# Gate projections computed with tokens on partitions and turned through DRAM, and a planner with other load times and finer tables

## The chip, the cores and the metric

The kernel runs on one core of a Trainium2 chip. The metric is device time in microseconds for one execution, here the median of three runs. All data is float32; the matmuls take operands split into a high and a low part (float32r), so that one product costs three matmuls.

## The reference, cut to what matters

Two layers act on 256 latent tokens of width 2048, with 256 context tokens beside them in the first. The first layer is the one that the change touches:

```python
p = h @ w_in                    # q, gate_a, z, k, v, xbc, dt
pc = hc @ w_in[:, base:]        # context: k, v, xbc, dt alone
ya = neighbourhood_attention(q, k, v, kc, vc, rpb) * jax.nn.silu(gate_a)
yb = gated_group_rmsnorm(y_ssd + d * lat[0], z, ssm_norm_g)   # uses y * silu(z)
out = jnp.concatenate([ya, yb], axis=-1) @ w_out
```

`gate_a` and `z` are 256 tokens by 2048 columns each. They exist for the latent tokens alone, while k, v and most of xbc exist for all 512. The attention output and the SSD output are kept with their channels on partitions and the tokens along the free dimension, so silu of both gates is needed in that layout too.

## The kernel before, in words

**Work and order.** The columns of the first projection are cut into four slices of 512 for each of q, gate (G), z (Z), k, v and x. The main program first runs a starting stage over eight pieces `j` of two 128-row blocks each: it makes the layer's modulation (`ada_gen`: small matmuls with `cpad`, then transposes, then A0 and S0), normalizes and modulates the tokens (`hH`, `hL`), and accumulates K, V, Q of slice 0 and B. Partial sums of K and V are added into `sz`, `gt` and `Vt`, which serve there as accumulators (`part_gen`, L830). Then come, slice by slice, `do_g`, `do_ssd`, `do_qk` and `do_gv`; heads of attention (`head_gen`) and SSD groups (`group_gen`) are emitted between the matmuls of the projections. The output projection and a second layer with a short convolution follow.

**Two forms of a projection.** `proj` calls `chunk`, which calls one of two forms for each 128-row block. `mm_ws` (kind 256 or 512) holds a 128x128 block of the weight and streams the tokens, so the result has channels on partitions. `mm_act` (kind "act") holds 128 tokens and streams 512 weight columns, so the result has tokens on partitions. For 256 tokens and a 512-column slice the first form takes, per row block, four column blocks by three matmuls of 256 columns; the second takes two token tiles by three matmuls of 512 columns. Q, K and V of the later slices run as "act" and are then turned: written to DRAM from the GpSimd queue (`kqd`, L1029), fetched back in 128-element pieces by four DMAs (`fetch`, L245) into the one buffer `PT0`, and transposed in 32x32 squares by VectorE (`blocks`, L250). The flag `dfree` hands out `PT0`, which the heads use as well for their probabilities.

**The gates before.** `do_g` and the end of `do_ssd` project G and Z with kind 256. `silu2_gen` (L1054) waits for `ok()`, which says that the previous slice's gate buffer is no longer read. Then it makes tanh on ScalarE (L1059), and on VectorE (L1061) it multiplies out of PSUM straight into `gt` or `sz`. Until `ok()` holds, the two PSUM banks of the projection stay taken.

**What sets the order.** While the program is written, the class `Plan` keeps a clock per engine and a time for each piece of each tile. A task is emitted where its inputs are ready by those clocks. Each engine then runs its instructions strictly in the order written. A load of weights is costed from its size and `RATE` and a fixed delay. Tables of times are kept in pieces of 128 elements (`keys`), so that two parts of `small` or `const` that are loaded at different times can share one entry. Weight loads are issued from SyncE (L428) whenever one of the buffers `raw` comes free; ScalarE makes the high part `wH` (L458), VectorE the low part `wL` (L465), up to three loads ahead of their use.

Of the kernel before, what the change touches and what calls it, by code (L numbers as in the profile page):

```python
# [10 lines left out]
AF = mybir.ActivationFunctionType  # L11
ALU = mybir.AluOpType
AX = mybir.AxisListType

D = 2048
KB = 16
EPS = 1e-6
COL_Q, COL_G, COL_Z, COL_K, COL_V, COL_X = 0, 2048, 4096, 6144, 8192, 10240
# [19 lines left out]
class Plan:  # L38


    NAMES = {"PE": "PE", "DVE": "DVE", "Activation": "ACT", "Pool": "POOL", "SP": "SP"}
    RATE = 270.0

    def __init__(self):
        self.t = dict.fromkeys(("PE", "DVE", "ACT", "POOL", "SP"), 0.0)
        self.w, self.r, self.last = defaultdict(float), defaultdict(float), defaultdict(float)
        self.dma = 0.0
        self.pool = (0.0, 0.0)

    def keys(self, ap):  # L50
        a, n = ap.ap, ap.tensor.name
        if type(ap.tensor).__name__ == "Tile" and not n.startswith("dram"):
            lo = ap.offset % a[0][0] if a[0][0] else ap.offset
            hi = lo + sum(abs(s) * (c - 1) for s, c in a[1:])
            return [(n, u) for u in range(lo // 128, hi // 128 + 1)]
        if n.startswith("in_") or n.startswith("out_"):
            return []
        hi = ap.offset + sum(abs(s) * (c - 1) for s, c in a)
        return [(n, u) for u in range(ap.offset // 256, hi // 256 + 1)]
# [38 lines left out]
    def add(self, b):  # L98
        i = b.ins
        e, op = self.NAMES[str(i.engine).split(".")[-1]], i.opcode  # L100
        ins = [x.bass_ap for x in i.ins if hasattr(x, "bass_ap")]
        outs = [x.bass_ap for x in i.outs if hasattr(x, "bass_ap")]
        ki, ko = [k for a in ins for k in self.keys(a)], [k for a in outs for k in self.keys(a)]
        s = self.t[e]
        for k in ki:
            s = max(s, self.w[k] + 60)
        for k in ko:
            s = max(s, 0.0 if e == "PE" or op == "DMACopy" else self.w[k] + 60, self.r[k] + 60)
        if op == "DMACopy":
            n = 4  # L110
            for _, c in outs[0].ap:
                n *= c
            self.t[e] = s + (1200 if e == "POOL" else 450)
            if e == "SP":
                self.dma = max(self.dma, s + 1000) + n / self.RATE
                done = free = self.dma + 1000
            else:
                done = free = max(self.dma, s + 1000) + n / self.RATE + 1500
            if any(a.tensor.name.startswith("dram") for a in ins + outs):
                done = free = done + 3000  # L120
        else:
            d, lat = self.cost(e, op, i, ins, outs)
            if e == "DVE" and not self.psum(ins + outs) and self.pool[0] <= s < self.pool[1]:
                s = self.pool[1]
            if e == "POOL":
                self.pool = (s, s + d)
            self.t[e] = s + d
            free, done = s + d, s + d + lat
        for k in ki:
            self.r[k] = max(self.r[k], free)  # L130
            self.last[k[0]] = max(self.last[k[0]], free)
        for k in ko:
            self.w[k] = max(self.w[k], done) if op == "DMACopy" else done
            self.last[k[0]] = max(self.last[k[0]], done)
        return b
# [36 lines left out]
def kernel(ctx: ExitStack, tc, x, cx, ada_w, ada_b, w_in, w_out, sc_in, sc_out, rpb, small, const,  # L172
# [8 lines left out]
    w_in, w_out, sc_in, sc_out = (Laid(w, n) for w, n in ((w_in, "w_in"), (w_out, "w_out"), (sc_in, "sc_in"), (sc_out, "sc_out")))  # L181
    V, S, G, T, DMA = nc.vector, nc.scalar, nc.gpsimd, nc.tensor, nc.sync
# [18 lines left out]
    def drt(shape, name):  # L201
        return dr.tile(list(shape), F32, name="dram_" + name)
# [38 lines left out]
    def fetch(dst, src):  # L241

        n = src.shape[0] // 32
        for b in range(4):
            E(G.dma_start(dst[32 * b:32 * b + 32].rearrange("p t (a x) -> p (t a) x", a=4),  # L245
                             bass.AP(tensor=src.tensor, offset=src.offset + 128 * b, ap=[[512, 32], [32 * 512, n], [1, 128]])))

    def blocks(o, i):

        E(V.transpose(o.rearrange("p k (a j) -> p a k j", a=4), i.rearrange("p (a k j) -> p a k j", a=4, k=4)))  # L250
# [7 lines left out]
    def spawn(q, gen, tmps=0, halves=0):  # L258
        q.append(Task(gen, tmps, halves))
# [127 lines left out]
    def give(pool, *bs):  # L387
        pool.extend(bs)
# [342 lines left out]
    def proj(nc_, kind, ps, nxt, leave=False):  # L731
        nb = 1024 // nc_
        for kb in range(0, KB, nb):
            if kb + 2 * nb >= KB:
                reserve[0] = nxt
            chunk(kb, kind, ps, kb == 0, kb + nb >= KB)
            if leave:
                free_rows[0] = kb + nb
        reserve[0] = 0
# [263 lines left out]
    def d_take(name):  # L1003
        dfree[0] = False
        return st([128, 2, 512], "PT0", name=name)
# [40 lines left out]
    def v_gen(a, ps):  # L1046
# [4 lines left out]
            give(free_b, ps[t])  # L1051
        got.add(("V", a))

    def silu2_gen(key, a, ps, dst, ok):  # L1054
        yield when(lambda: ok())
        for b in range(2):
            yield W_("ACT", ps[b])
            th = tmp()
            E(S.activation(th, ps[b], AF.Tanh, scale=0.5))  # L1059
            yield W_("DVE", th)  # L1060
            E(V.scalar_tensor_tensor(out=dst[:, 2 * b:2 * b + 2, :].rearrange("p b c -> p (b c)"), in0=th, scalar=1.0,  # L1061
                                     in1=ps[b], op0=ALU.add, op1=ALU.mult))
            give(free_t, th)
            give(free_b, ps[b])
        got.add((key, a))

    b0 = rpbs[0, :, :]
# [6 lines left out]
    def head_gen(a, h):  # L1074
# [59 lines left out]
        yield W_("POOL", ptd[hd])  # L1134
        give(free_t, sps[0], sps[1])
        yield ("cap", 0, 0)
        yield when(lambda: dfree[0] and (hd == 0 or ("d", hd - 1) in got))
        Dt = d_take(f"D{hd}")
        got.add(("d", hd))
        yield W_("POOL", ptd[hd])  # L1140
# [383 lines left out]

    def do_g(a, nxt):
        psG = banks(2)
        proj(512, 256, psG, nxt)
        spawn(urgent, silu2_gen("G", a, psG, gt, lambda: attn[0] >= 8 * a and (a or ("K", 0) in got)), 1)

    def do_ssd(s, nxt):  # L1530
        if s:
            psB = banks(2)
            proj(256, 512, psB, 1)
            spawn(urgent, make_b(s, psB), 3)
        psC, = banks(1)
        proj(256, 256, [psC], 4)
        spawn(urgent, make_c(s, psC), 0, 2)
        psX = banks(4)
        proj(512, 512, psX, 2)
        for gi in range(2):  # L1540
            spawn(urgent, make_x(s, gi, psX[2 * gi:2 * gi + 2]), 3)
        psZ = banks(2)
        proj(512, 256, psZ, nxt)
        spawn(urgent, silu2_gen("Z", s, psZ, sz, lambda: ssd_done[0] >= 2 * s and ("K", 0) in got), 1)
        for gi in range(2):
            spawn(side, group_gen(s, gi), 3, 4)

# [456 lines left out]
```

## Time and profile before

| | |
|---|---|
| three runs | 1768.23, 1772.86, 1772.92 us; median 1772.86 |
| profiled execution | 1762.67 us; span of its instructions 1760.9 us |
| granted TensorE clock, mean | 0.999 |
| TensorE busy | 1728.3 us, 98% of the span |
| VectorE, ScalarE, GpSimd busy | 1292.8, 785.3, 191.0 us |
| moved by DMA | 412.50 MB, mean 234 GB/s |

A row of the profile names engine, line, operation, and output and input tiles with buffer numbers left out. For a matmul the moving operand is named first: `bank<-hH,wH 128x256` streams 256 tokens against a held block of the weight, and `bank<-wH,hH 128x512` streams 512 weight columns against 128 held tokens. Matmuls are pipelined, so the time from one row's start to the next row's start tells their pace, and the duration of a row is longer than that. A bracket behind a row of the timeline gives the engine's idle time ahead of it and the engine that ended it.

### The profile page before, as it was taken

How to read it: one execution, taken by the hardware profiler on the slowest of the kernel's cores; microseconds unless marked ns; L12 is line 12 of the kernel's file. 1: busy time of each engine (PE TensorE's matmuls, PEld its weight loads, DVE VectorE, ACT ScalarE, POOL GpSimd, SP SyncE). 2: the span in 40 equal slices, each digit the busy share in tenths (PEclk: the TensorE clock that was granted, in tenths of full speed). 3: DMA queues.
4: the chain of work that ended last, by engine and by line, in shares of the span. 5: the costliest groups of instructions: out<-in, count | busy, mean ns of one | idle time of the engine just before them, and what ended most of it. 6: DMA issues, size and time to landing. Idle time of an engine off the chain costs nothing.

```text
span 1760.9 us, 25272 instructions
## 1 busy us (share of the span) xinstructions
PE 1728.3 (98%) x9305; PEld 1442.4 (82%) x9305; DVE 1292.8 (73%) x2041; ACT 785.3 (45%) x1186; POOL 191.0 (11%) x300
## 2 busy tenths in 40 slices
PE   6999999999999999999999999999999999999998
PEld 4677988889888889888888898888878888888887
DVE  5566877888787987786888698876667776766555
ACT  5422335454354453353453444654435444444442
POOL 0000111013111012111012101110000000000000
PEclk9999999999999999999999999999999999999999
DMA  9987675577876677866577767787766888876774
GB/s 349 344 291 252 214 227 181 181 214 241 261 227 201 190 219 248 262 193 204 170 239 227 215 188 226 224 261 253 268 216 232 265 281 266 267 248 216 219 231 158
DMA packets 147629, 412.50 MB, mean 234 GB/s; under 512 B 34304, under 2 KB 48272, under 8 KB 147504
## 3 DMA queue, kind: packets, MB, share of 16 engines
q1 hardware_dynamic: 132112, 366.64, 64.0%
q0 software_dynamic: 15392, 44.24, 8.0%
q8 instruction: 73, 1.20, 0.3%
q14 instruction: 52, 0.43, 0.1%
HBM read 386.53 MB, written 25.59 MB: 234 GB/s over the span
## 4 chain that ended last, share of the span: by engine, by line
PE 94%; DVE 2%; DMA 1%; ACT 1%; issue 1%; SPq 0%; POOL 0%; DVEq 0%; ACTq 0%; POOLq 0%
PE bank L231 93%; PE bank L235 1%; DVE wL L465 1%; DMA raw<-in_ada_w 0%; ACT wH L458 0%; DMA half<-in_rows 0%; DVE hL L804 0%; SPq L618 0%; DMA raw<-in_sc_in 0%; DVE tmp L1283 0%; DVE h L1729 0%; DVE tmp L800 0%; ACT h L1748 0%; ACT hH L798 0%; DVE xm L664 0%
## 5 line engine op out<-in xcount | busy, mean ns | idle before, releaser
L458 ACT CAST wH<-raw 128x1024 fp32r<-128x1024 f32 (+1 forms) x440 | 459.5, 1045 | 664.0 <-PE bank L231 559.6
L465 DVE TENSOR_TENSOR wL<-raw,wH 128x1024 fp32r<-128x1024 f32 (+1 forms) x440 | 532.2, 1213 | 257.4 <-ACT wH L458 255.0
L231 PE MATMUL bank<-hH,wH 128*128 128x256 f32 (+1 forms) x1040 | 341.0, 328 | 0.9 <-ACT wH L458 0.9
L231 PE MATMUL bank<-hL,wH 128*128 128x256 f32 (+1 forms) x1040 | 337.0, 324 | 0.0
L231 PE MATMUL bank<-hH,wL 128*128 128x256 f32 (+1 forms) x1024 | 331.4, 324 | 3.1 <-DVE wL L465 3.1
L231 PE MATMUL bank<-wH,h 128*128 128x512 f32 x1024 | 316.8, 390 | 1.7 <-DVE h L1729 1.7
L231 PE MATMUL bank<-wH,hH 128*128 128x512 f32 x640 | 256.0, 400 | 4.8 <-ACT hH L798 2.6
L231 PE MATMUL bank<-wL,hH 128*128 128x512 f32 x640 | 249.9, 391 | 0.3 <-DVE wL L465 0.3
L231 PE MATMUL bank<-wH,hL 128*128 128x512 f32 x640 | 249.3, 390 | 0.1
L231 PEld LDWEIGHTS bank<-wH,h 128*128 128x128 f32 x1024 | 191.9, 188 | 43.5 <-DVE h L1729 3.0
L231 PEld LDWEIGHTS bank<-hH,wH 128*128 128x128 f32 x1040 | 197.8, 190 | 18.9 <-issue 2.0
L231 PEld LDWEIGHTS bank<-hL,wH 128*128 128x128 f32 x1040 | 197.8, 190 | 15.8
L231 PEld LDWEIGHTS bank<-hH,wL 128*128 128x128 f32 x1024 | 194.6, 190 | 19.4 <-DVE wL L465 4.1
L857 DVE SCALAR_TENSOR_TENSOR acc<-raw,csil,acc 128x512 f32<-128x512 f32 x240 | 179.1, 746 | 30.9 <-DMA raw<-in_ada_w 27.2
L231 PE MATMUL bank<-wL,h 128*128 128x512 f32 x512 | 199.4, 389 | 0.2 <-DVE wL L465 0.2
L231 PE MATMUL bank<-wH,mix 128*128 128x512 f32 x512 | 160.9, 391 | 0.0
L231 PEld LDWEIGHTS bank<-wH,hH 128*128 128x128 f32 x640 | 120.1, 188 | 36.3 <-issue 7.2
L231 PEld LDWEIGHTS bank<-wH,hL 128*128 128x128 f32 x640 | 120.1, 188 | 25.4 <-DVE hL L804 0.6
L231 PEld LDWEIGHTS bank<-wL,hH 128*128 128x128 f32 x640 | 120.1, 188 | 25.0 <-DVE wL L465 1.1
L231 PEld LDWEIGHTS bank<-wL,h 128*128 128x128 f32 x512 | 96.1, 188 | 20.6 <-DVE wL L465 0.6
L231 PEld LDWEIGHTS bank<-wH,mix 128*128 128x128 f32 x512 | 96.1, 188 | 20.4 <-issue 0.5
L231 PE MATMUL bank<-wL,mix 128*128 128x512 f32 x256 | 99.7, 390 | 0.0
(276 smaller groups left out, 1856.5 us busy)
## 6 DMA issues: line engine op xcount, KB each, us to landing
raw<-in_w_in SPq DMA_DIRECT2D x209, 512.0 KB
raw<-in_ada_w SPq DMA_DIRECT2D x163, 512.0 KB
raw<-in_sc_in SPq DMA_DIRECT2D x128, 512.0 KB
raw<-in_w_out SPq DMA_DIRECT2D x64, 512.0 KB
raw<-in_sc_out SPq DMA_DIRECT2D x32, 512.0 KB
dram_ptd<-tmp POOLq DMA_DIRECT2D x32, 256.0 KB, 4.9
D<-dram_ptd POOLq DMA_DIRECT2D x64, 128.0 KB, 5.6
tmp<-dram_csr SPq DMA_DIRECT2D x32, 256.0 KB
```

The costliest lines, as they stand in the source:

```text
L231: E(T.matmul(o, l, r, start=start, stop=stop, skip_group_check=True))
L235: E(T.transpose(o, i, ident if k == 128 else ident[:k, :k]))
L458: E(S.copy(H, v))
L465: E(V.tensor_tensor(out=Lo, in0=v, in1=H.bitcast(F32), op=ALU.subtract))
L857: E(V.scalar_tensor_tensor(out=acc, in0=v[:, j], scalar=csil[:, 2 * k + j:2 * k + j + 1], in1=acc, op0=ALU.mult, op1=ALU.add))
```

## The change

The change has two parts. The first is about the gates. G and Z are projected with kind "act", so the two PSUM banks hold 128 tokens each. `silu2_gen` no longer waits first: it makes tanh and the product at once into a temporary of 128 tokens by 512 columns, gives its banks back, and writes the temporary to a new DRAM tensor `gzd` from the GpSimd queue. After that it waits for `ok()` and for `dfree`, takes `PT0`, fetches the turned gate with four DMAs on the GpSimd queue, and VectorE transposes two halves into `gt` or `sz`. The columns of the G and Z weights are permuted ahead of the launch, so the product needs no rearranged access. A head now also waits for its slice's G before it takes `PT0`.

The second part is about the planner. `RATE` rises from 270 to 400 bytes per ns, and the fixed delay of a load grows from 1000 + 1000 to 1500 + 2500 ns. At most ten loads from SyncE are in flight in the plan. The tables of `small` and `const` are kept in pieces of two elements instead of 128.

```diff
-    RATE = 270.0
+    RATE = 400.0
...
+        self.land = []
...
-            return [(n, u) for u in range(lo // 128, hi // 128 + 1)]
+            k = 2 if n.startswith(("small", "const")) else 128
+            return [(n, u) for u in range(lo // k, hi // k + 1)]
...
+            if e == "SP" and len(self.land) >= 10:
+                s = max(s, self.land[-10])
             self.t[e] = s + (1200 if e == "POOL" else 450)
             if e == "SP":
-                self.dma = max(self.dma, s + 1000) + n / self.RATE
-                done = free = self.dma + 1000
+                self.dma = max(self.dma, s + 1500) + n / self.RATE
+                done = free = self.dma + 2500
+                self.land.append(done)
...
+    gzd = drt([8, 256, 512], "gzd")
+
     def silu2_gen(key, a, ps, dst, ok):
-        yield when(lambda: ok())
-        for b in range(2):
-            yield W_("ACT", ps[b])
+        ths = []
+        src = gzd[4 * (key == "Z") + a]
+        for t in range(2):
+            yield W_("ACT", ps[t])
             th = tmp()
-            E(S.activation(th, ps[b], AF.Tanh, scale=0.5))
+            E(S.activation(th, ps[t], AF.Tanh, scale=0.5))
             yield W_("DVE", th)
-            E(V.scalar_tensor_tensor(out=dst[:, 2 * b:2 * b + 2, :].rearrange("p b c -> p (b c)"), in0=th, scalar=1.0,
-                                     in1=ps[b], op0=ALU.add, op1=ALU.mult))
-            give(free_t, th)
-            give(free_b, ps[b])
+            E(V.scalar_tensor_tensor(out=th, in0=th, scalar=1.0, in1=ps[t], op0=ALU.add, op1=ALU.mult))
+            give(free_b, ps[t])
+            yield W_("POOL", th)
+            E(G.dma_start(src[t * 128:(t + 1) * 128], th))
+            ths.append(th)
+        yield W_("POOL", src)
+        give(free_t, *ths)
+        yield ("cap", 0, 0)
+        yield when(ok)
+        yield when(lambda: dfree[0])
+        Dt = d_take(f"D{key}{a}")
+        yield W_("POOL", src)
+        fetch(Dt, src)
+        for t in range(2):
+            yield W_("DVE+", Dt)
+            blocks(dst[:, :, t * 128:(t + 1) * 128], Dt[:, t])
+        dfree[0] = True
         got.add((key, a))
...
-        yield when(lambda: dfree[0] and (hd == 0 or ("d", hd - 1) in got))
+        yield when(lambda: dfree[0] and ("G", a) in got and (hd == 0 or ("d", hd - 1) in got))
...
-        proj(512, 256, psG, nxt)
-        spawn(urgent, silu2_gen("G", a, psG, gt, lambda: attn[0] >= 8 * a and (a or ("K", 0) in got)), 1)
+        proj(512, "act", psG, nxt)
+        spawn(urgent, silu2_gen("G", a, psG, gt, lambda: attn[0] >= 8 * a and (a or ("K", 0) in got)), 2)
...
-        proj(512, 256, psZ, nxt)
-        spawn(urgent, silu2_gen("Z", s, psZ, sz, lambda: ssd_done[0] >= 2 * s and ("K", 0) in got), 1)
+        proj(512, "act", psZ, nxt)
+        spawn(urgent, silu2_gen("Z", s, psZ, sz, lambda: ssd_done[0] >= 2 * s and ("K", 0) in got), 2)
...
+    w_in[:, COL_G:COL_K] = w_in[:, COL_G:COL_K].reshape(D, 8, 4, 4, 32).transpose(0, 1, 3, 2, 4).reshape(D, 4096)
```

The order of the instructions moves almost everywhere, since every decision of the planner rests on its clocks. Three places matter for what follows. The first is TensorE where the projection of gate slice 0 begins, behind the last matmuls of B. Before:

```order
L231 MATMUL bank_129<-hH_1441,wH_141 128x512
L231 MATMUL bank_129<-hL_1446,wH_141 128x512
L231 MATMUL bank_129<-hH_1441,wL_144 128x512
L231 MATMUL bank_127<-hH_366,wH_142 128x256
L231 MATMUL bank_127<-hL_370,wH_142 128x256
L231 MATMUL bank_127<-hH_366,wL_145 128x256
```

Now:

```order
L236 MATMUL bank_129<-hH_1423,wH_141 128x512
L236 MATMUL bank_129<-hL_1428,wH_141 128x512
L236 MATMUL bank_129<-hH_1423,wL_144 128x512
L236 MATMUL bank_133<-wH_142,hH_366 128x512
L236 MATMUL bank_133<-wL_145,hH_366 128x512
L236 MATMUL bank_133<-wH_142,hL_370 128x512
L236 MATMUL bank_127<-wH_142,hH_366 128x512
L236 MATMUL bank_127<-wL_145,hH_366 128x512
L236 MATMUL bank_127<-wH_142,hL_370 128x512
```

The operands have changed places and each matmul streams 512 columns. A gate slice has 96 of them where it had 192; over the whole program 1536 matmuls of 256 columns go and 768 of 512 come. C keeps the old form (384 of 256 columns).

The second place is VectorE in the starting stage, while TensorE works on piece 1 and the modulation of piece 2 is made (`S`, then `hL`; `sz` and `gt` are the sums that free PSUM banks). Before:

```order
L830 TENSOR_TENSOR sz<-sz,bank_127 128x512
L830 TENSOR_TENSOR sz<-sz,bank_128 128x512
L776 TENSOR_REDUCE S_214<-bank_133 128x4
L782 TENSOR_TENSOR S_214<-S_214,small 128x4
L800 TENSOR_SCALAR tmp_112<-xm_200,A_213,S_214 128x256 x2
L804 TENSOR_TENSOR hL_700<-tmp_112,hH_695 128x512
L800 TENSOR_SCALAR tmp_113<-xm_201,A_213,S_214 128x256 x2
L804 TENSOR_TENSOR hL_707<-tmp_113,hH_702 128x512
L465 TENSOR_TENSOR wL_143<-raw_139,wH_140 128x1024
L830 TENSOR_TENSOR gt<-gt,bank_134 128x512
```

Now:

```order
L835 TENSOR_TENSOR sz<-sz,bank_127 128x512
L781 TENSOR_REDUCE S_214<-bank_128 128x4
L787 TENSOR_TENSOR S_214<-S_214,small 128x4
L805 TENSOR_SCALAR tmp_112<-xm_200,A_213,S_214 128x256 x2
L809 TENSOR_TENSOR hL_693<-tmp_112,hH_688 128x512
L805 TENSOR_SCALAR tmp_113<-xm_201,A_213,S_214 128x256 x2
L809 TENSOR_TENSOR hL_700<-tmp_113,hH_695 128x512
L470 TENSOR_TENSOR wL_143<-raw_139,wH_140 128x1024
L835 TENSOR_TENSOR sz<-sz,bank_133 128x512
L835 TENSOR_TENSOR gt<-gt,bank_134 128x512
```

The block of `S` and `hL` stands one sum earlier, and the transposes on TensorE that feed `S` stand six projection matmuls earlier. In the next piece the four matmul groups with `cpad` that feed the following modulation stand 21 rows earlier on TensorE (row 198 instead of 219). Before that, the transposes of the third token tile stand six matmuls earlier, and at the very start the first 32 matmuls with `cpad` stand together ahead of the transposes of `xs` instead of on both sides of them.

The third place is the GpSimd queue behind the writes of K and Q of slice 0 (`fetch` of K and Q, then what follows). Before:

```order
L245 DMA kqD_K_1984<-dram_kqd 32x8x128 x4
L245 DMA kqD_K_2139<-dram_kqd 32x8x128 x4
L245 DMA kqD_Q_2228<-dram_kqd 32x8x128 x4
L1268 DMA dram_csr<-tmp_112 64x256
L1269 DMA dram_exr<-tmp_112 64x256
L869 DMA dram_mrow<-rowb 4x128
```

Now:

```order
L250 DMA kqD_K_1888<-dram_kqd 32x8x128 x4
L1072 DMA dram_gzd<-tmp_112 128x512
L1072 DMA dram_gzd<-tmp_114 128x512
L250 DMA kqD_K_2034<-dram_kqd 32x8x128 x4
L250 DMA kqD_Q_2104<-dram_kqd 32x8x128 x4
L250 DMA DG_2167<-dram_gzd 32x8x128 x4
L1289 DMA dram_csr<-tmp_117 64x256
L1290 DMA dram_exr<-tmp_117 64x256
```

The two writes of G stand between the two fetches of K, and its fetch stands behind that of Q, ahead of the SSD rows `csr` and `exr`.

More of the change, by code (lines that the diff above doesn't have):

```diff
@@ L1982 @@
     strict = np.stack([lt.T, lt], axis=1)
+    w_in = np.array(f('na_ssd_w_in')[0])
+    w_in[:, COL_G:COL_K] = w_in[:, COL_G:COL_K].reshape(D, 8, 4, 4, 32).transpose(0, 1, 3, 2, 4).reshape(D, 4096)
     def laid(w, name):
@@ L1987 @@
     arr = {
-        'x': f('x')[0], 'cx': f('ctx')[0], 'ada_w': np.concatenate([laid(f('ada_w')[k], f'ada_{k}') for k in range(2)]), 'ada_b': f('ada_b'), 'w_in': laid(f('na_ssd_w_in')[0], 'w_in'),
+        'x': f('x')[0], 'cx': f('ctx')[0], 'ada_w': np.concatenate([laid(f('ada_w')[k], f'ada_{k}') for k in range(2)]), 'ada_b': f('ada_b'), 'w_in': laid(w_in, 'w_in'),
         'w_out': laid(f('na_ssd_w_out')[0], 'w_out'),
```

## The prediction

> **What bounds the kernel now.** I read the page first, for the shares of the engines and the chain that ended last.
>
> ```profile
> span 1760.9 us, 25272 instructions
> ...
> PE 1728.3 (98%) x9305; PEld 1442.4 (82%) x9305; DVE 1292.8 (73%) x2041; ACT 785.3 (45%) x1186; POOL 191.0 (11%) x300
> ...
> PE 94%; DVE 2%; DMA 1%; ACT 1%; issue 1%; SPq 0%; POOL 0%; DVEq 0%; ACTq 0%; POOLq 0%
> ```
>
> TensorE is busy for 98% of the span and carries 94% of the chain. A busy share can hide slow matmuls, so the question is where the other 32.6 us lie (1760.9 less 1728.3). The busy times by stretches of 50 us tell that; the columns are length, PE, PEld, DVE, ACT, POOL, granted clock, DMA share and GB/s.
>
> ```profile
> 0.00:50.00 50.00, 32.85 (x257) 22.74 (x258) 27.30 (x82) 28.64 (x65) 3.13 (x11) 1.00 0.94 356
> 50.00:100.00 50.00, 46.64 (x321) 32.88 (x320) 30.03 (x57) 16.72 (x30) 0.00 (x0) 1.00 0.86 317
> 100.00:150.00 50.00, 50.00 (x341) 36.95 (x340) 32.15 (x58) 17.05 (x27) 0.00 (x0) 1.00 0.86 300
> 150.00:200.00 50.00, 49.66 (x267) 39.02 (x266) 34.23 (x53) 12.90 (x17) 0.00 (x0) 1.00 0.57 193
> 200.00:250.00 50.00, 47.67 (x352) 45.26 (x352) 40.39 (x59) 24.20 (x35) 12.39 (x16) 1.00 0.82 262
> ...
> 550.00:600.00 50.00, 49.49 (x318) 43.98 (x317) 40.59 (x65) 22.20 (x32) 3.62 (x7) 1.00 0.60 191
> ...
> 1100.00:1150.00 50.00, 49.39 (x243) 40.56 (x242) 41.35 (x88) 33.15 (x72) 5.25 (x8) 1.00 0.69 218
> ```
>
> TensorE idles 17.2 us in the first stretch, 3.4 in the second, 2.3 between 200 and 250, and 0.3 to 0.6 in three others. So beyond the start the time is the sum of the matmuls' paces. A change gains here by fewer TensorE cycles, or in the first 100 us by shorter waits; it loses by any wait that it puts in front of TensorE.
>
> **The gates' matmuls.** What the change removes is one form and what it adds is another; both are in the trace.
>
> ```profile
> L231 PE MATMUL bank<-hH,wH 128*128 128x256 f32 x640 | 183.3, 286 | 0.0
> L231 PE MATMUL bank<-hH,wL 128*128 128x256 f32 x640 | 181.4, 284 | 2.8 <-DVE wL L465 2.8
> L231 PE MATMUL bank<-hL,wH 128*128 128x256 f32 x640 | 181.0, 283 | 0.0
> L231 PE MATMUL bank<-wH,hH 128*128 128x512 f32 x640 | 256.0, 400 | 4.8 <-ACT hH L798 2.6 <-DVE sz L830 1.5 <-DVE gt L830 0.8
> ```
>
> The 1920 matmuls of 256 columns are G and Z (8 slices by 192) and C (384). The means of 286 and 400 ns are latencies of overlapping instructions and can't be multiplied by the counts. The pace is read from starts in the timeline: first the whole projection of gate slice 0, 192 matmuls from the first row to the start of the third, then an unbroken run of 60 matmuls of the other form.
>
> ```profile
> 200.95 0.28 PE L231 MATMUL bank<-hH,wH 128*128 128x256 f32 x1
> ...
> 223.86 0.28 PE L231 MATMUL bank<-hH,wL 128*128 128x256 f32 x1
> 223.98 0.40 PE L231 MATMUL bank<-hH,wH 128*128 128x512 f32 x1
> ```
>
> ```profile
> 357.10 0.39 PE L231 MATMUL bank<-wH,hH 128*128 128x512 f32 x1
> ...
> 370.49 0.39 PE L231 MATMUL bank<-wH,hL 128*128 128x512 f32 x1
> ```
>
> A gate slice takes 23.03 us now, 120.0 ns a matmul. The other form runs at 13.39 us over 59 steps, 227.0 ns. Twice the columns cost less than twice the time, as if each matmul paid a fixed 13 ns (2 x 120.0 less 227.0). A slice of 96 such matmuls takes 21.79 us, so each slice saves 1.24 us and the eight save 9.9 us. The end of the range on one side is the fixed part read a little differently (226.4 ns gives 10.4 us). On the other side, this form restarts more slowly after a small matmul: the mean of the first kind of three, 400 ns, stands 10 above the others. If every one of the 32 groups per slice paid 10 ns more, it would lose 2.6 us of the 9.9, so 7.3 to 10.4.
>
> [...]
>
> **The way through DRAM.** The same turn is in the trace for K and Q; these are its rows.
>
> ```profile
> L245 POOL DMA_DIRECT2D kqD_K<-dram_kqd x32 | 18.6, 588 | 78.1 <-DVE KT L250 37.2 <-DVE tmp L1209 23.7 <-DVE QT L250 10.2
> L1029 POOL DMA_DIRECT2D dram_kqd<-tmp x24 | 13.4, 559 | 19.1 <-DVE tmp L1024 13.4 <-DMA tmp<-dram_csr 2.2 <-DVE tmp L1464 1.7
> L250 DVE STREAM_TRANSPOSE KT<-kqD_K 128x512 f32<-128x512 f32 x16 | 10.5, 691 | 6.0 <-DMA kqD_K<-dram_kqd 6.0
> dram_kqd<-tmp POOLq DMA_DIRECT2D x24, 256.0 KB, 4.7
> kqD_K<-dram_kqd POOLq DMA_DIRECT2D x32, 128.0 KB, 5.6
> ```
>
> A gate adds two writes and four fetches on GpSimd (2 x 0.56 + 4 x 0.59 = 3.5 us of queue) and two transposes (1.4 us of VectorE). The eight add 28 us to GpSimd's 191 and 11 us to VectorE's 1293. Tanh and product stay 16 and 16. I cost all of it at nothing, because TensorE has work meanwhile and neither engine is near full. What counts is the delay of one gate: issue, 4.7 us landing, issue, 5.6 us landing, two transposes, together 15.2 us. Its readers are the end of a head (L1170) and of an SSD group (L1481). Behind G stands V with its 192 matmuls (43.6 us at 227.0 ns) in slices 1 to 3. Behind Z stands the next slice's Q (21.8 us) or, for the last, G and V. So the cover is 21.8 us or more against 15.2. If it went, each gate would cost up to 15.2 us. On the GpSimd queue the gates' DMAs now stand ahead of fetches for heads; a head behind one waits 3.5 us longer, which the planner's order leaves room for. The DMA engines move 8.4 MB more (8 x 1 MB), 2% of 412.5. In stretches with a DMA share of 0.6 to 0.8 that delays weight loads by a few us. The three prepared loads cover that, since one lasts TensorE 12 matmuls, 2.7 us.
>
> What goes: two PSUM banks no longer wait for `ok()`. TensorE doesn't wait for a bank in this stage of the trace, so that is worth nothing directly.
>
> **The order.** The planner takes 5.3 us for a 512 KB load where it took 3.9 (4.0 us plus 524288 bytes by 400, against 2.0 plus the same by 270), but lets loads follow closer. In the starting stage three waits of TensorE, the second to fourth row here, hang on the order of VectorE and ScalarE.
>
> ```profile
> 13.11 2.29 PE L231 MATMUL bank<-raw,cpad 128*32 128x256 f32 x16 [13.11 <-DVE rx L606]
> ...
> 36.63 0.50 PE L231 MATMUL bank<-wH,hH 128*128 128x512 f32 x1 [1.36 <-ACT hH L798]
> ...
> 69.03 0.50 PE L231 MATMUL bank<-wH,hH 128*128 128x512 f32 x1 [0.79 <-DVE gt L830]
> ...
> 89.06 0.50 PE L231 MATMUL bank<-wH,hH 128*128 128x512 f32 x1 [1.47 <-DVE sz L830]
> ```
>
> ```profile
> 68.29 0.68 DVE L830 TENSOR_TENSOR gt<-gt,bank 128x512 f32<-128x512 f32 x1
> 88.32 1.28 DVE L830 TENSOR_TENSOR sz<-sz,bank 128x512 f32<-128x512 f32 x2
> ```
>
> The first is shortened if the transposes of the third token tile stand six matmuls (1.36 us) earlier. The second and third are waits for a bank that a sum frees late, because `S`, `hL` and `wL` stand ahead of it on VectorE; the new order has that block earlier. At most 3.6 us go. But the matmuls with `cpad` now want their loads up to 21 matmuls (4.8 us) sooner, and with DMA shares of 0.94 and 0.86 in these stretches some of them will not have landed; what is late next is then the load. The other end is therefore 2 us lost. I take half of the 3.6, a gain of 1.8 us. The 13.1 us ahead of the first matmul stay, since the loads ahead of it keep their order.
>
> One wait does not move. At 235 us VectorE stops for a small load of `rows`, and TensorE's 2.3 us between 200 and 250 follow from it.
>
> ```profile
> 242.40 0.43 DVE L1203 TENSOR_TENSOR half<-half,half 128x256 f32<-128x256 f32 x1 [6.09 <-DMA half<-in_rows]
> ```
>
> In the new order the same two instructions stand next to each other, so it stays. New waits elsewhere: the old order has 1.5 us of them past 150 us beside this one (0.34, 0.51 and 0.61 in the stretches above). A fully reshuffled order can have none or several times that, 0 to 5 us; I add 0.7 us.
>
> Sum: -9.9 - 1.8 + 0.7 = -11.0 us. The profiled execution of 1762.67 us would become 1751.7. It lies 10.2 us under the median of the three runs, and the runs themselves span 4.7 us. Against the median the forecast is 1772.86 - 11.0 = 1761.9 us. A change under 0.3% (5.3 us) is about what a measurement of this kernel can't tell from none, so faster means below 1767.5 and slower above 1778.2.
>
> **The rivals.**
> - *Larger gain* (0.14). All 3.6 us of the start go, VectorE's stop for `rows` falls into cover (2.3 us), and no new wait comes: -9.9 - 3.6 - 2.3 = -15.8, about 1757. For it speaks that the plan's load times are nearer to what loads take; against it that the order around `rows` is unchanged.
> - *The order eats it* (0.15). 6 to 11 us of new waits spread over the program, from an order that trusts 400 bytes per ns where the first stretch moved 356: about 1768 to 1773, the same. Against it: three loads of cover.
> - *Slower* (0.08). A gate is late. TensorE, which takes head and SSD matmuls strictly in order, stands still until `gt` or `sz` frees or the shared `PT0` comes back. The point is 1.4 us per gate (11.0 by 8); at 3 us per gate, 24 us, the time is 1786. For it: `PT0` has 8 more users of some 15 us each, and heads now wait for G. Against it: the same turn for K and Q costs TensorE next to nothing now: of the stretches between 250 and 1100 us only the one at 550 has any idle time, 0.5 us.
> [...]
>
> **How the numbers follow.** The forecast has 0.60. Faster is 0.60 + 0.14 = 0.74, same 0.15 + 0.03 = 0.18, slower 0.08. The range goes from the forecast counted from the profiled execution (1751.7, rounded to 1751) up into the case where the order eats most of the gain (1771).
>
> **What would show it.** In the new profile the 256-column rows should count 384 and the 512-column rows of `wH,hH` 896; a gate projection's 96 matmuls should take 21.8 us without a break. The waits near 36, 68 and 88 us should be shorter or gone, VectorE should still stop some 6 us for `rows`. TensorE should stay at 98% busy with its sum about 10 us lower. I am wrong if waits of TensorE for `PL`, `sz` or `y` appear past 250 us, if waits for `raw` appear in the first 150 us, or if the 512-column gate matmuls run slower than 230 ns.

## The result and the profile after

The changed kernel takes 1773.32 us (median of 22 runs, 1764.03 to 1779.43) against 1769.97 us for the kernel before on the same chips (22 runs, 1765.04 to 1776.19). The ratio is 1.0026, with a 95% interval of 1.0016 to 1.0036: 4.6 us slower, inside the 0.3% that the prediction took as no change, and not the 1761.9 us that it forecast. Two profiles are compared below, and they lie at opposite ends: the one of before is quicker than all its 22 timed runs (1762.67 us), the one after is the slowest of its 22 (1779.43 us). Their difference of 16.8 us is therefore too large by some 12, but it shows where the time goes.

The page after gives TensorE's busy time and the chain that ended last.

```profile
span 1777.7 us, 23854 instructions
...
PE 1731.6 (97%) x8537; PEld 1406.6 (79%) x8537; DVE 1300.5 (73%) x2057; ACT 784.6 (44%) x1186; POOL 220.2 (12%) x348
...
PE 52%; DMA 4%; DVE 4%; issue 1%; ACT 1%; POOL 0%; SPq 0%; DVEq 0%; ACTq 0%
```

TensorE runs 768 matmuls fewer and yet is busy 3.3 us longer, and it idles 46.1 us (1777.7 less 1731.6) where it idled 32.6. The shares of the chain can't be set against those of before: this chain can be followed back only to 689 us, and they add up to 62% of the span. The forms and the pace are as foreseen. The first fence has two groups by form, the second the first gate projection: its first row and the row after its last.

```profile
L236 PE MATMUL bank<-wH,hH 128*128 128x512 f32 x896 | 359.4, 402 | 2.3 <-ACT hH L803 1.5 <-DVE sz L835 0.8
...
L236 PE MATMUL bank<-hH,wL 128*128 128x256 f32 x128 | 37.0, 289 | 1.9 <-DVE wL L470 1.9
```

```profile
198.87 0.39 PE L236 MATMUL bank<-wH,hH 128*128 128x512 f32 x1
...
220.63 0.39 PE L236 MATMUL bank<-hH,wH 128*128 128x512 f32 x1
```

96 matmuls in 21.76 us, 226.7 ns each: 1.27 us less than the 23.03 of before, 10.2 us for eight gates if the others do the same. So the gain is there. The stretches of 50 us tell where it is given back (length, PE, PEld, DVE, ACT, POOL, granted clock, DMA share, GB/s).

```profile
0.00:50.00 50.00, 33.33 (x257) 22.11 (x258) 27.26 (x83) 28.77 (x65) 3.13 (x11) 1.00 0.93 353
50.00:100.00 50.00, 48.07 (x352) 33.17 (x351) 31.09 (x64) 18.99 (x33) 0.00 (x0) 1.00 0.96 359
...
200.00:250.00 50.00, 48.10 (x257) 41.93 (x256) 41.02 (x59) 24.04 (x37) 13.79 (x18) 0.97 0.82 257
...
400.00:450.00 50.00, 46.31 (x217) 37.20 (x216) 37.98 (x65) 22.53 (x40) 15.94 (x22) 0.97 0.80 234
450.00:500.00 50.00, 49.20 (x230) 39.83 (x231) 37.85 (x68) 19.64 (x31) 15.35 (x26) 0.97 0.78 250
...
650.00:700.00 50.00, 46.75 (x232) 36.64 (x231) 37.92 (x75) 25.84 (x54) 7.38 (x7) 1.00 0.72 219
...
1100.00:1150.00 50.00, 45.25 (x199) 36.53 (x198) 34.26 (x69) 28.08 (x61) 11.13 (x17) 0.93 0.74 232
```

The start idles 18.6 us where it idled 20.5. Everything behind it idles 27.5 us where it idled 12.1. And the granted clock falls below 1.00 in four of these stretches, which it did nowhere between 50 and 1750 us of before. Behind the first wait for `rx`, 13 us in both kernels, the waits of TensorE that are longest in total (total, times, longest) are these two now and this one before:

```profile
PE bank L236 <- DVE tmp L1488: 9.6, 5, 3.2
PE bank L236 <- DVE wL L470: 8.5, 10, 1.9
```

```profile
PE bank L231 <- DVE wL L465: 3.6, 5, 2.3
```

The waits for `wL`, the low part of a weight, grow by 4.9 us. Wholly new is the other line: five waits for the SSD masks (`tmp`, L1488), which VectorE makes and the matmuls of `py` stream. One of them step by step, first on VectorE, then on TensorE.

```profile
403.49 0.71 DVE L1166 STREAM_TRANSPOSE D<-D 128x512 f32<-128x512 f32 x1 [2.12 <-DMA D<-dram_ptd]
...
406.40 0.42 DVE L1488 TENSOR_TENSOR tmp<-tmp 128x256 f32<-128x256 f32 x1
```

```profile
406.87 0.65 PE L236 MATMUL bank<-tmp,xtm 128*64 128x128 f32 x6 [1.87 <-DVE tmp L1488]
...
408.32 0.63 PE L236 MATMUL bank<-wH,hH 128*128 128x512 f32 x1
408.75 0.63 PE L236 MATMUL bank<-wL,hH 128*128 128x512 f32 x1
```

VectorE runs its instructions in the order written: the ten rows that are listed for the starting stage lie in this trace in that order, from 59.05 to 67.42 us. Here it stands still 2.12 us for a head's fetch that has not landed and then works without a break up to the mask, which is late by as much; TensorE waits 1.87 us. Then it pays again: for 3.41 us a 512-column matmul starts every 0.43 us and not every 0.227. The granted clock of that piece (same columns as above):

```profile
408.15:411.45 3.30, 3.30 (x10) 2.51 (x9) 3.27 (x6) 0.41 (x1) 0.83 (x1) 0.50 0.71 207
```

Eight matmuls at 0.2 us more make 1.6 us, as an estimate. There are five such pieces in this execution, 8.0 us, and they count as busy: this is why the busy time did not fall. The three other long mask waits (ending at 450.8, 665.8 and 1127.8 us) stand behind a stop for another DMA, the load of a modulation matrix for the next layer, whose step (L862) nobody needs yet. VectorE has no idle time between these stops and the masks either, which end 5 to 10 us later:

```profile
445.58 1.54 DVE L862 SCALAR_TENSOR_TENSOR acc<-raw,csil,acc 128x512 f32<-128x512 f32 x2 [4.70 <-DMA raw<-in_ada_w]
```

```profile
660.06 1.54 DVE L862 SCALAR_TENSOR_TENSOR acc<-raw,csil,acc 128x512 f32<-128x512 f32 x2 [3.78 <-DMA raw<-in_ada_w]
```

```profile
1117.58 0.75 DVE L862 SCALAR_TENSOR_TENSOR acc<-raw,csil,acc 128x512 f32<-128x512 f32 x1 [7.84 <-DMA raw<-in_ada_w]
```

The sum of the two profiles: -10.2 (forms) - 1.9 (start) + 15.4 (idle behind it) + 8.0 (half clock) = +11.3 of the 16.8; the other 5.5 us count as busy, in many small delays between matmuls that no row names.

### The profile page after: what moved, and what is told of

Read it like the earlier page. It is cut to its first block, busy times and chain, and to the rows that moved or that the text cites. A ratio compares the mean times of both kernels' runs of the same rounds, so it can differ in the third digit from the quotient of the medians.

```text
span 1777.7 us, 23854 instructions
## 1 busy us (share of the span) xinstructions
PE 1731.6 (97%) x8537; PEld 1406.6 (79%) x8537; DVE 1300.5 (73%) x2057; ACT 784.6 (44%) x1186; POOL 220.2 (12%) x348
## 4 chain that ended last, share of the span: by engine, by line
PE 52%; DMA 4%; DVE 4%; issue 1%; ACT 1%; POOL 0%; SPq 0%; DVEq 0%; ACTq 0%
PE bank L236 51%; DMA raw<-in_ada_w 2%; DVE wL L470 1%; DMA kqD_K<-dram_kqd 1%; PE bank L240 0%; DMA tmp<-in_x 0%; ACT wH L463 0%; DMA D<-dram_ptd 0%; DVE acc L862 0%; DVE KT L255 0%; POOL kqD_K L250 0%; DVE tmp L1304 0%; DVE tmp L1661 0%; DVE h L1750 0%; ACT h L1769 0%
## 5 line engine op out<-in xcount | busy, mean ns | idle before, releaser
L236 PE MATMUL bank<-wH,hH 128*128 128x512 f32 x896 | 359.4, 402 | 2.3 <-ACT hH L803 1.5
L236 PE MATMUL bank<-wL,hH 128*128 128x512 f32 x896 | 351.3, 392 | 2.6 <-DVE wL L470 2.4
L236 PE MATMUL bank<-wH,hL 128*128 128x512 f32 x896 | 350.6, 392 | 0.1
L862 DVE SCALAR_TENSOR_TENSOR acc<-raw,csil,acc 128x512 f32<-128x512 f32 x240 | 179.3, 747 | 28.5 <-DMA raw<-in_ada_w 24.8
L236 PEld LDWEIGHTS bank<-wL,hH 128*128 128x128 f32 x896 | 169.1, 189 | 39.0 <-DVE wL L470 4.7
L236 PE MATMUL bank<-hH,wH 128*128 128x512 f32 (+1 forms) x528 | 195.0, 369 | 0.9 <-ACT wH L463 0.9
L236 PE MATMUL bank<-hL,wH 128*128 128x512 f32 (+1 forms) x528 | 192.9, 365 | 0.0
L236 PE MATMUL bank<-hH,wL 128*128 128x512 f32 (+1 forms) x512 | 187.0, 365 | 2.2 <-DVE wL L470 2.2
L236 PEld LDWEIGHTS bank<-hH,wH 128*128 128x128 f32 x528 | 100.3, 190 | 17.8 <-issue 1.4
L236 PEld LDWEIGHTS bank<-wH,mix 128*128 128x128 f32 x512 | 97.4, 190 | 20.8 <-issue 0.7
L236 PEld LDWEIGHTS bank<-hL,wH 128*128 128x128 f32 x528 | 100.4, 190 | 15.2
L236 PEld LDWEIGHTS bank<-hH,wL 128*128 128x128 f32 x512 | 97.3, 190 | 18.3 <-DVE wL L470 2.8
```

Source lines behind the costliest of these rows:

```text
L236: E(T.matmul(o, l, r, start=start, stop=stop, skip_group_check=True))
L862: E(V.scalar_tensor_tensor(out=acc, in0=v[:, j], scalar=csil[:, 2 * k + j:2 * k + j + 1], in1=acc, op0=ALU.mult, op1=ALU.add))
```

## The experiments

Each ratio is to the kernel before, run on the same chip. The theories by letter: P, the new plan's order makes the waits; D, later G, the gates' way through DRAM makes them; R, later S, any other order makes them. Q, Z, W and F are explained where they are first used.

**The two halves apart, before once more, and a nudge.** `e0` is the kernel before. `e1` is the changed kernel with the old plan, `e2` the old kernel with the new plan. `e3` is the changed kernel with

```diff
-    RATE = 400.0
+    RATE = 405.0
```

> The kernel before once more, to see what a usual execution of it shows: the profiled one took 1762.67 us, less than any of the 22 timed ones (1765.04 to 1776.19, median 1769.97). Every theory expects a ratio of 1.000. If the 7 us between profile and median are stretches at half clock, as the changed kernel's profile has five of 3.41 us after waits of 2 us (1.6 us each), then its runs show a granted clock of 0.996 to 0.998 and not 0.999; if they are DMA weather, the clock stays at 0.999 and the time still spreads.

> Only the gates are changed (their form, the turn through DRAM, the columns of the weights); the plan has its old loads, delays and tables. Theory P (the new plan's order makes the new waits, the gates themselves cost nothing): the 9.9 us of the forms come in full, 1758 to 1762 us, ratio 0.994 to 0.996, and no wait of TensorE over 1 us for the SSD masks past 250 us. Rival D (the gates' way through DRAM makes them: their fetches hold the one buffer and GpSimd's queue, heads and masks come late): about the changed kernel's time, 1770 to 1775, with the same waits for masks. Rival R (any reshuffled order gets several us of new waits, whatever shuffled it): 1762 to 1772, with waits at other places than the changed kernel's.

> Only the plan is changed (rate, delays, ten loads under way, tables apart); the gates are as before. Theory P: the new waits without the gain, 13 us worse than before less the 2 at the start: 1778 to 1784, ratio 1.005 to 1.008, waits for SSD masks as in the changed kernel. Rival D: no such waits and the gain of the start, 1767 to 1770, ratio 0.998 to 1.000. Rival R: 1768 to 1780, waits at other places.

> The changed kernel with the planner's rate at 405 bytes per ns instead of 400, a change of 1.2% in one number, which no load notices by itself but which moves instructions on every engine. Theory P and rival D have a cause that this leaves in place: within 3 us of the changed kernel (1770 to 1776), waits at the same steps of the program. Rival R (waits are the luck of an order): over 4 us away to either side, 1760 to 1769 or above 1777, the five waits for masks gone or at other groups.

Measured: e0 1.0008 (0.9996 to 1.0020), its runs at a mean granted clock of 0.997 to 1.000, those at 0.999 alone from 1767.29 to 1772.26 us, so half-clock stretches explain the spread of before at most in part; e1 1.0048 (1.0034 to 1.0062); e2 0.9999 (0.9988 to 1.0010); e3 1.0001 (0.9991 to 1.0011). Theory P falls: the plan alone costs nothing, the gates alone cost 8.5 us. e1 is slower than every range put down for it, and its longest waits behind the start are not for the masks that D named:

```profile
PE bank L231 <- DVE wL L465: 5.9, 10, 2.1
PE bank L231 <- ACT Vt L1050: 4.6, 1, 4.6
```

And e3 says that a number which means nothing moves the time by 4.4 us, so one order proves little. The runs of before average a clock of 0.998, those after 0.9956. By the clock alone that is, as an estimate, 0.0025 x 1773 = 4.4 us; but e3 averages 0.9959 and is as quick as before, so the clock alone does not decide.

**The gates without their way.** `e5` goes straight from the banks into the gate's tile; `e6` adds the six DMAs, unawaited. In both the banks wait for `ok()` first, as in the kernel before, and the exchange between the 32-partition blocks is left out, so the gates hold other numbers.

```diff
-            yield W_("POOL", th)
-            E(G.dma_start(src[t * 128:(t + 1) * 128], th))
-            ths.append(th)
...
-        fetch(Dt, src)
...
+            yield W_("DVE", th)
+            blocks(dst[:, :, t * 128:(t + 1) * 128], th)
+            give(free_t, th)
```

> The changed kernel without the way through DRAM: the gate, projected with tokens on partitions, goes from its banks through tanh, product and VectorE's transposes straight into its tile, as soon as that is free. What it leaves out: blocks are turned within their 32 partitions only and not exchanged between them, so the gates hold other numbers. TensorE's work and VectorE's are those of the changed kernel; GpSimd's six DMAs per gate and the hold of the shared buffer are gone. Theory D (the way through DRAM makes the waits): 9.9 us of the forms and some 2 of the start come in, 1756 to 1761 us, ratio 0.993 to 0.996. Rival R (any reshuffled order has its several us): 1762 to 1772. Rival F (the forms gain nothing): 1768 or more, with no new waits.

> As the kernel without the way through DRAM, but each gate also issues its six DMAs on GpSimd (two writes of 256 KB, four reads of 128 KB in the fetch's pattern, into DRAM and not into the shared buffer), and nobody waits for them. The same is left out as there. It tells GpSimd's queue and the DMA traffic from the hold of the shared buffer and the delay. Theory D in the form that the hold and the delay cost: within 3 us of the kernel without the way, 1756 to 1763. Theory D in the form that GpSimd's queue or the traffic costs (6 x 0.58 us of GpSimd ahead of a head's fetch): 1766 to 1773.

Measured: e5 0.9964 (0.9950 to 0.9977), e6 0.9995 (0.9982 to 1.0008). The waits of e5:

```profile
PE bank L236 <- DVE wL L470: 3.2, 4, 2.6
...
PE bank L236 <- DVE tmp L1473: 1.5, 1, 1.5
```

Masks 1.5 us where the changed kernel has 9.6. In this order 6.4 us are gained. That is just short of the range of theory D (0.993 to 0.996) and inside the one of R (1762 to 1772 us), so it does not part the two. e6 lies between e5 and the changed kernel, 5.5 us from each, which is hardly more than the scatter.

**One gate at a time.** `e7` has only Z in the new form, `e8` only G; the other keeps the old form, and in e7 heads do not wait for G.

> The changed kernel with only the SSD gate Z in the new form and through DRAM; the attention gate G is as before and heads wait for it no earlier than before. Half of the forms' gain, 5 us, is left. Theory D in the form that heads wait for G: the waits go, 1762 to 1765. In the form that any gate holds the shared buffer between heads: half the waits, 1767 to 1770. Rival R: 1762 to 1773, no pattern.

> The changed kernel with only the attention gate G in the new form and through DRAM; Z is as before. Theory D in the form that heads wait for G, whose fetch can only begin when the last head of the slice before has used the gate: nearly all of the new waits stay with half of the gain, 1772 to 1778. In the form that any gate holds the buffer: 1767 to 1770. Rival R: 1762 to 1773, no pattern.

Measured: e7 1.0023 (1.0011 to 1.0036), e8 0.9987 (0.9974 to 1.0000). The form in which heads wait for G falls. Of the other form of D, 1767 to 1770 us for both, e8 keeps to it (1768.2) and e7 does not (1772.8). Z, which I thought the harmless one, loses 4 us with half the gain, and its longest wait is for a mask:

```profile
PE bank L236 <- DVE tmp L1501: 7.9, 5, 3.7
```

**The late gate.** In the changed trace Z is late, on GpSimd and then on VectorE:

```profile
322.16 0.61 POOL L1072 DMA_DIRECT2D dram_gzd<-tmp  x1 [28.00 <-DVE tmp L1069]
325.85 0.54 POOL L1072 DMA_DIRECT2D dram_gzd<-tmp  x1 [3.08 <-DVE tmp L1069]
...
351.97 2.56 POOL L612 TENSOR_TENSOR statq<-statq,const 128x8 f32<-128x8 f32 x1 [14.06 <-DVE statq L611]
354.49 2.37 POOL L250 DMA_DIRECT2D DZ<-dram_gzd  x4
```

```profile
364.59 1.30 DVE L255 STREAM_TRANSPOSE sz<-DZ 128x512 f32<-128x512 f32 x2
```

From the first write to the last transpose 43.7 us pass, not 15.2, while in the kernel before `sz` was complete at 324 us: the fetch stands in GpSimd's order behind a step for `statq` that itself waits 14.06 us for VectorE. `e9` lets the SSD group start without Z; `e10` is that at rate 405, `e11` that with the old plan. `e12` is the kernel before with the groups held.

```diff
-        yield when(lambda: all(k in got for k in (("X", s, 0), ("X", s, 1), ("Z", s))))
+        yield when(lambda: all(k in got for k in (("X", s, 0), ("X", s, 1))))
...
+            yield when(lambda: ("Z", s) in got)
+            yield W_("DVE", y, sz[:, 2 * gi + b, :])
```

```diff
+        zt.setdefault(s, plan.t["PE"])
+        yield when(lambda: plan.t["PE"] >= zt[s] + 30000)
```

> The changed kernel, but an SSD group starts when X is there and no longer waits for the gate Z; only its last product, y by sz, does. In the changed kernel's trace sz is complete at 365, 638, 890 and 1077 us against 324, 611, 858 and 1045 before, since the fetch waits for the shared buffer, and the groups' masks come that much later and bunched. Theory Z (the late gate holds the groups back, and bunched masks make TensorE wait): most of the waits for masks go (9.6 us with their half-clock stretches 16), 1758 to 1764 us, ratio 0.993 to 0.997. Rival Q (GpSimd's queue and the DMA traffic of the gates make the waits): little changes, 1769 to 1775. Rival R (the luck of an order): 1762 to 1773.

> The same with the planner's rate at 405 instead of 400, to have a second order of the same kernel. Theory Z: within 3 us of the one with 400 and 1758 to 1764. Rival R: 4 us or more away from it; the mean of the two then stands against the mean of the changed kernel with 400 and 405 (1.0026 and 1.0001).

> The gates alone with the old plan (ratio 1.0048), with the groups' earlier start. Theory Z: 8 us or more faster than without it, 1761 to 1768, ratio 0.996 to 1.000. Rival Q: 1773 to 1778 still. Rival R: anything between.

> The kernel before, its gates by the old way, with one thing added: an SSD group starts 30 us of the planner's TensorE time after its X and Z are there, as late as the late gate makes it. Nothing is left out of the computation and nothing goes through DRAM. Theory Z: waits for masks appear and the time rises by 5 to 12 us, 1774 to 1781, ratio 1.003 to 1.007. Rival Q: no wait, ratio 0.999 to 1.001. Rival R: up to 8 us slower, but with waits at other places than masks.

Measured: e9 1.0052 (1.0038 to 1.0067), e10 1.0058 (1.0042 to 1.0074), e11 1.0014 (1.0005 to 1.0023), e12 1.0076 (1.0058 to 1.0095). The same edit costs 4.6 us at 400, 10 at 405, and gains 6 with the old plan. Theory Z falls in this form, and e9 is above all three ranges: the groups' first matmuls start at 359, 634, 896 and 1083 us in e9, at 363, 636, 900 and 1089 in the changed kernel and at 346, 617, 881 and 1071 before, so Z was not what held them. e12 is slow, as Z asked, but its longest waits are not for masks:

```profile
PE bank L231 <- DVE wL L465: 10.1, 8, 4.1
PE bank L231 <- DVE tmp L1471: 3.7, 3, 2.9
```

**Is it only the order?** `e13` and `e14` nudge the order of before alone, to 275 and 265 instead of 270. `e15` lets a gate of the changed kernel hold one tmp tile; `e16` reserves two in the kernel before.

```diff
-            ths.append(th)
-        yield W_("POOL", src)
-        give(free_t, *ths)
+            yield W_("POOL", src[t * 128:(t + 1) * 128])
+            give(free_t, th)
```

```diff
+        z0 = plan.t["PE"]
+        yield when(lambda: plan.t["PE"] >= z0 + 12000)
```

> The kernel before with the planner's rate at 275 instead of 270 bytes per ns: a neutral nudge that moves instructions on every engine and changes nothing else. Rival S (the order of before is a favoured one, and any other order of the same work costs several us): 4 to 10 us slower, ratio 1.002 to 1.006. Theory G (the gates' way through DRAM costs by its holds): within 3 us, ratio 0.998 to 1.002.

> The same to the other side, 265 instead of 270. Rival S: ratio 1.002 to 1.006 again. Theory G: 0.998 to 1.002. The three orders of before and the orders with the gates at 270, 400 and 405 (1.0048, 1.0026, 1.0001) then give the scatter that an order alone makes.

> The changed kernel, but a gate holds one tmp tile and not two: the second token tile starts when the first one's write has landed. Ten tmp tiles serve all work; the X tiles of an SSD slice, two groups of five, are what wants them just when Z's gate holds two. Theory G with the tmp tiles as the place: 5 us or more faster than the changed kernel, 1762 to 1768, ratio 0.996 to 0.9995. With the shared buffer as the place: 1770 to 1775. Rival S: 1766 to 1778, no pattern.

> The kernel before, its gates by the old way, but each gate reserves two of the ten tmp tiles instead of one, from its start to 12 us of the planner's TensorE time after its product. Nothing goes through DRAM. Theory G with the tmp tiles as the place: 5 to 10 us slower, ratio 1.003 to 1.006, X and the masks later. With the shared buffer as the place: no change beyond the scatter of an order, 0.998 to 1.002.

Measured: e13 1.0068 (1.0052 to 1.0084), e14 1.0026 (1.0014 to 1.0038), e15 0.9992 (0.9979 to 1.0005), e16 1.0043 (1.0029 to 1.0056). A change of 2% in one number of the planner, with no change of the work, costs the kernel before 12 us to one side, more than rival S asked, and 4.6 to the other. So an order alone can cost more than the whole change does. It need not: e2 is a third new order of the same work, and it costs nothing. The trace of e13 (VectorE, then TensorE) has one wait of the kind found above, 3.06 us of the 12, now without any gate in DRAM:

```profile
404.07 0.75 DVE L857 SCALAR_TENSOR_TENSOR acc<-raw,csil,acc 128x512 f32<-128x512 f32 x1 [3.85 <-DMA raw<-in_ada_w]
404.74 0.42 DVE L1490 TENSOR_TENSOR half<-half,half 128x256 f32<-128x256 f32 x1
```

```profile
405.21 1.01 PE L231 MATMUL bank<-const,half 128*128 128x1 f32 x4 [3.06 <-DVE half L1490]
```

Of three other orders of before two are slower, one is equal and none is quicker. So the order of before looks like a favoured one, and a kernel with another order may give up that favour; three orders are few to say it by. e15 and e16 move as the tmp tiles ask (-6 us against the changed kernel, +7.6 against before), but by no more than nudges do; which hold it is stays open.

**More distance.** `e17` (changed kernel) and `e18` (e15) make TensorE take heads' and groups' matmuls later behind their operands:

```diff
-            return rdy + (0 if isurg else 800) <= now + 100
+            return rdy + (0 if isurg else 3000) <= now + 100
```

> The changed kernel with one number of the planner changed: TensorE takes the matmuls of heads and SSD groups only when their operands are, by the plan, 3.0 us old and no longer 0.8. The new waits are of that kind: 9.6 us for masks and the half-clock stretches behind them, since in the trace VectorE runs 2 us behind the plan where it stops for a fetch. Theory W (each new order leaves a few such steps closer to their operands than the trace's delays allow, and that is where the time goes): the waits for masks mostly go, 5 to 10 us faster than the changed kernel, 1762 to 1768, ratio 0.996 to 0.9995. Rival S alone (an order's luck, not the distance of these steps): 1768 to 1782, no better than the other orders with the gates (0.9992 to 1.0058).

> The same number in the kernel whose gates hold one tmp tile (0.9992): the best candidate for a version ahead of both. Its profile has one wait of 4.6 us for masks at 1103 us with a half-clock stretch, 6.4 us together. Theory W: 1760 to 1765, ratio 0.995 to 0.998. Rival S alone: 1768 to 1780.

Measured: e17 1.0195 (1.0181 to 1.0210), e18 0.9972 (0.9963 to 0.9982). The waits of e17, and its stretch at the layer's end:

```profile
PE bank L236 <- DVE wL L470: 19.2, 16, 8.0
...
PE bank L236 <- DVE acc L862: 11.9, 1, 11.9
PE bank L240 <- DMA rowb<-dram_mrow: 5.7, 1, 5.7
PE bank L236 <- DVE half L1737: 4.1, 1, 4.1
...
PE bank L236 <- DVE tmp L1488: 1.6, 2, 0.9
```

```profile
1300.00:1350.00 50.00, 28.30 (x132) 23.60 (x131) 21.60 (x33) 10.94 (x18) 2.71 (x4) 0.74 0.51 169
```

The masks' waits fall from 9.6 to 1.6 us as theory W said. But other waits come in their place: at the layer's end TensorE waits 11.9 us for the modulation (`acc`) that the next layer needs, it waits 19.2 us for `wL` in all, and the whole is 34 us behind the kernel before, far outside the ranges of W and S. In e18 these waits are small:

```profile
PE bank L240 <- DMA rowb<-dram_mrow: 3.4, 1, 3.4
PE bank L236 <- DVE acc L862: 3.3, 1, 3.3
PE bank L236 <- DVE tmp L1486: 1.6, 1, 1.6
```

e18 leaves nothing out and is quicker than both kernels: 5 us ahead of before, 9.6 of the changed kernel by the ratios. Whether its edits did that or its order's luck, one order cannot say.

## Why the prediction was wrong

**The forms: right.** 21.76 us a slice where 21.79 was forecast, 10.2 us in all for 9.9. A matmul of 512 columns took 226.7 ns after, one of 256 took 120.0 ns before.

**The start: right.** 1.9 us less idle for 1.8 forecast. Two waits for `raw`, 0.2 us each at 16 and 17 us, are all that came of the loads feared there.

**The stop for `rows`: right as a wait, wrong in what it costs.**

```profile
238.60 0.42 DVE L1224 TENSOR_TENSOR half<-half,half 128x256 f32<-128x256 f32 x1 [6.13 <-DMA half<-in_rows]
```

It stayed, 6.13 us for 6.09, and TensorE idles 1.9 us for 2.3. But here a piece at half clock followed (0.97 in that stretch), and in the profile of before none did. The last section has what parts the two in the traces: here the wait leaves TensorE idle for 0.56 of one step of 3.413 us, while the longer one of before, on the grid of the one half-clock piece of that profile (at 1758.5 us), is cut by a border into 0.38 and 0.30. So, as an estimate from these two, this part of the loss is the luck of where a wait falls.

**The way through DRAM at nothing: wrong.** The step read the path of one gate as a sum of its own pieces, 15.2 us. Queue positions were not in it: Z took 43.7 us in the slice shown and 24 to 27 in the other three, G 43.7, 32.4, 31.5 and 20.8. TensorE never waited for `gt` or `sz` behind the start, so the cover held in the narrow sense. What it costs comes out only over several orders. Without the way, the kernel before at four settings of the plan (270, 275, 265, the new one) averages 1.0023 (1.0000, 1.0068, 1.0026, 0.9999); with it, the changed kernel at three (old plan, 400, 405) averages 1.0025 (1.0048, 1.0026, 1.0001). The forms alone should put the second 0.0056 lower (9.9 of 1770), so the way costs about 0.0058, 10 us. The single ratios scatter by 0.003, so this is an estimate, good to some 4 us, from few orders. e5 (0.9964, where 1.0023 - 0.0056 = 0.9967 would be expected) agrees with it.

**The new order at +0.7 us (0 to 5): with the way at nothing, this is the step that failed.** By the ratio, the change costs 4.6 us where the forms and the start give 12.1, so 16.7 us came on top, where these two terms had 0.7 together. Of these some 10 are the way's, by the estimate above, and the rest is what another order costs: 0, 4.6 and 12 us in the three other orders of before. How the 16.7 divide between the two stays open within some 4 us. I counted the waits that the old order had and took the new order to be of the same kind. But the old one was no fair sample: with its rate moved by 2%, it gets worse to both sides. The count was short as well: it left out TensorE's idle 2.7 us between 1300 and 1350 us and 5.6 us at the end; the changed kernel has these too (3.2 and 5.5 us), so this did not move the forecast.

**The rivals.** "The order eats it" (0.15, 1768 to 1773) comes nearest, at 1773.3, but in its number more than in its mechanism. It laid the waits to a plan that trusts 400 bytes per ns, and with that plan alone e2 loses nothing (0.9999), while without it e1 is at 1.0048. I spoke against it with the three loads of cover, and waits of TensorE for loads indeed hardly came; they came through VectorE, which I had only looked at for `rows` and in the start. The named sign "waits for `PL`, `sz` or `y`" did not appear; one step ahead of `y`, at its masks, it did. The 0.03 in the sum for "same" stood for a smaller gain of the forms, a term that no run shows; the runs showed 1.27 us a slice, 10.2 us for eight.

**What joins the runs.** In the 20 profiles, TensorE has 77 waits of 1 us or more between 150 and 1300 us. 63 of them (136 of 169 us) end within 12 us behind the end of a stop of VectorE of 1 us or more for a DMA that had not landed: a modulation load, a head's fetch, `rows`, a turned K. Such 12 us cover only 14% of the time. The profile of before has 16 such stops and after 13, so what differs between these two is not their number but what stands behind them. Over all profiles the number does go with the time: eight have 7 to 13 stops and ratios of 0.9964 to 1.0026 (mean 0.9992; e18 with 7 and e5 with 8 are the two quickest kernels), twelve have 14 to 21 and ratios of 1.0000 to 1.0195 (mean 1.0051). This is read from one profile of each; no kernel was made to take these stops away and change nothing else, so as a cause it is argued and not shown.

## What to carry to other kernels

A tuned order is a selected one: before costing a change to what a scheduler is fed, move one of its neutral numbers a little, a few times, and judge the change against that scatter and not against the one tuned time. In an in-order engine that waits for DMAs, ask of each such wait what stands behind it and who needs that. And a path through queues is as long as the queue positions make it, not as the sum of its own steps: here up to 43.7 us where the steps add up to 15.2.

## What the runs showed of the hardware

The half-clock pieces of the trace after begin on one grid of 3.413 us: five of that length, at a granted clock of 0.50, begin at 240.9, 408.2, 452.5, 1128.4 and 1138.6 us, and the later four lie 49, 62, 260 and 263 such steps behind the first. Laid on that grid, TensorE's idle share in the step just ahead of them was 0.56, 0.55, 0.50, 0.57 and 0.54; in each of these steps ends a wait of 1.8 to 2.2 us. At the program's end, the steps with 1.00 idle (after, from 1773.5 us) and 0.93 (before, from 1755.1 us) had a half-clock piece behind them too. The other steps past 100 us with 0.30 or more, at 0.47, 0.47, 0.41 and 0.38 in the trace after and at 0.42, 0.38 and 0.30 in that of before, were followed by a clock of 1.00. So the wait of 3.18 us that ends at 665.8 us, which a border cuts into 0.47 and 0.47, cost no clock, and the one of 1.87 us at 406.9, all in one step (0.55), did. Each such piece costs some 1.6 us beside the wait, by the estimate above from the starts 0.43 and 0.227 us apart. This is read from two executions, and no run was made to move a wait across a border and change nothing else.
